# Attention weights times values as three passes of split operands, and negated scores whose minimum is taken, in a hybrid attention/GLA decoder trunk

## The chip, the cores and the metric

One core of one Trainium2 chip runs the whole program. The metric is the device time of one execution in microseconds (us), as the median over runs; smaller is better. Engine names are those of the profile: PE is the matrix engine, PEld its weight loads, DVE the vector engine, ACT the scalar engine, POOL and SP the other two.

## What is computed

Four residual layers over 1,040 tokens (16 learned meta tokens ahead of 1,024 real ones) of width 1,024 in float32: differential attention, squared-ReLU MLP, gated linear attention, MLP. The change touches the attention layer alone. Cut to that:

```python
def diff_attention(x, w_in, lam_params, subln_w, w_out, lambda_init):
    q, k, v = jnp.split(x @ w_in, [D_MODEL, 2 * D_MODEL], axis=-1)
    # 8 heads; q and k have two components of 64, v has 128 columns per head
    for s, e in bounds:          # 16 meta rows, then 8 blocks of 128 rows
        scores = jnp.einsum('bqhcd,bkhcd->bhcqk', qb, kb) * scale
        scores = jnp.where(dist >= 0.0, scores - slopes * dist, -jnp.inf)
        p = jax.nn.softmax(scores, axis=-1)
        attn = p[:, :, 0] - lam * p[:, :, 1]
        outs.append(jnp.einsum('bhqk,bkhe->bqhe', attn, vb))
    o = rmsnorm(o, subln_w) * (1.0 - lambda_init)
    return o.reshape(B, L, DA_HEADS * DA_V_DIM) @ w_out
```

## The kernel before, in words

The projections of a head (`att_project`, L385) are products in three passes of split operands: a float32 operand is kept as a rounded part in the type F32R and the F32R remainder, and `mm3` (L185) multiplies high by high, low by high and high by low, lines L190, L191 and L192, in chunks of 348, 346 and 346 columns. The scores of row block i (`Head.score`, i = 0 to 8) are two F32R passes per chunk, L421 and L422: K split into KH and KL, against Q with both halves of its split stacked in the 128 rows. A DVE custom instruction (L424) adds the distance table `nsd` and carries the running maximum; L428 negates the maximum; ACT takes the exponential with the sum beside it (L429); L433 to L435 combine the two components into `e`.

`Head.turn` then transposes `e` in blocks of 128 keys on PE (L453, four to a PSUM bank of the tag `tp`, which has two banks) and ACT copies each bank to a tile `pt` (L454). `Head.av` multiplies: for each key block one plain float32 product `pt` by `V` of 128x128 (L469), and one with the meta values `Vm` (L467), summed in the one bank of the tag `o`. Block i has i + 1 such products, so a head has 45 and the eight heads 360. DVE copies the result to `osb` (L473), ACT sums its squares (L474). After blocks 3 and 8, `norm` scales by the root mean square (L484), transposes back (L492) and spills a split copy to DRAM (`spill`, L393 to L396), to be read for the output projection.

The heads are pipelined. In the main loop each row block runs the steps "FSFSFAT": F is a third of a chunk of the next head's projection, S half of the scores, A the `av` of the block turned in the step before, T the next `turn`. The Tile framework then orders the instructions of every engine by itself, so rows of different lines interleave on PE. `turn` takes its `pt` tiles from the pool `tmp` of four buffers, which `norm` uses too.

The whole program is ordered in this way: attention until about 548 us of the span, the output projection, MLP (L1066, L898), GLA, MLP.

Of the kernel before, what the change touches and what calls it, by code (L numbers as in the profile page):

```python
# [8 lines left out]
F32 = mybir.dt.float32  # L9
# [7 lines left out]
P = 128  # L17
# [33 lines left out]
def tile_hybrid_trunk(ctx, tc, hT, win, lamp, wout, gwin, gwz, gwup, gwout, wup, wdn, wdl,  # L51
# [219 lines left out]
    def small_rs(ssq, add, cnt, lo, hi):  # L271
        w = mpool.tile([P, 16], F32, tag="nrm_w", name=nm("nw"))
        r = mpool.tile([P, 16], F32, tag="nrm_r", name=nm("nr"))
        t = mpool.tile([P, 16], F32, tag="nrm_t", name=nm("nt"))
# [12 lines left out]
        return r  # L287
# [79 lines left out]
        return KH, KL  # L367

    def turn_v(h, v):
        V = slot(16 + 8 * (h % 2) + 6, "V", F32, (P, 8, P))  # L370
        Vm = mpool.tile([P, P], F32, tag="vm", name=nm("vm"))
        nc.gpsimd.memset(Vm, 0.0)
        for g in range(2):
            tp = psum("tp")
            for j in range(4):
                kb = 4 * g + j
                nc.tensor.transpose(tp[:, j * P:(j + 1) * P], v[:, NMETA + kb * P:NMETA + (kb + 1) * P], ident)
            nc.scalar.copy(V[:, 4 * g:4 * g + 4, :].rearrange("p a b -> p (a b)"), tp)
        tp = psum("tp")
        nc.tensor.transpose(tp[:NMETA, :P], v[:, 0:NMETA], ident)  # L380
        nc.scalar.copy(Vm[:NMETA], tp[:NMETA, :P])
        return V, Vm

    def att_project(h, R):
        q = slot(32, "qst")  # L385
        yield from proj(xs, CH3, ev_scaled(q, 0.125), bank_pj, lambda: R.update(Q=split_q(h, q)), cuts=(3, 5))
# [11 lines left out]
    class Head:  # L398
        def __init__(self, h, R):
            self.h, self.R = h, R  # L400
            self.sums = mpool.tile([P, 2, 9], F32, tag="sums", name=nm("sums"))
            self.ssq = mpool.tile([P, 9], F32, tag="ssq", name=nm("ssq"))
            self.e, self.pt, self.osb = {}, {}, {}

        def score(self, i):
            if i == 0 and self.h > 0:
                nc.scalar.mul(nsd, nsd, 0.5)
            Q, (KH, KL), sums = self.R["Q"], self.R["K"], self.sums
            nk = NMETA + P * i
            off = 912 if i == 0 else 1024 - P * i  # L410
            q0 = 0 if i == 0 else NMETA + P * (i - 1)
            e = [slot(34 + 2 * (i % 3) + c, "e") for c in range(2)]
            st4 = mpool.tile([P, 16], F32, tag="mx", name=nm("mx"))
            mx = st4[:, 0:8].rearrange("p (c j) -> p c j", j=4)
            nmx, rho = st4[:, 8:10], st4[:, 10:12]
            chs = col_chunks(nk)
            for c in range(2):
                for j, (c0, n) in enumerate(chs):
                    ps = psum("s")
                    w = n  # L420
                    nc.tensor.matmul(ps[:, :w], Q[c][:, q0:q0 + P], KH[c][:, c0:c0 + w], start=True, stop=False)  # L421
                    nc.tensor.matmul(ps[:, :w], Q[c][:, q0:q0 + P], KL[c][:, c0:c0 + w], start=False, stop=True)  # L422
                    last = j == len(chs) - 1
                    nc.vector.tensor_tensor_reduce(  # L424
                        e[c][:, c0:c0 + n], ps[:, :n], nsd[:, off + c0:off + c0 + n], 1.0,
                        -3.0e38 if j == 0 else mx[:, c, j - 1:j], ALU.add, ALU.max,
                        mx[:, c, 3:4] if last else mx[:, c, j:j + 1])
                nc.vector.tensor_scalar(nmx[:, c:c + 1], mx[:, c, 3:4], -1.0, None, ALU.mult)  # L428
                nc.scalar.activation(e[c][:, :nk], e[c][:, :nk], AF.Exp, bias=nmx[:, c:c + 1],  # L429
                                     accum_out=sums[:, c, i:i + 1])  # L430
                if c == 0:
                    yield
            nc.vector.reciprocal(rho[:, 0:1], sums[:, 1, i:i + 1])  # L433
            nc.vector.scalar_tensor_tensor(rho[:, 1:2], sums[:, 0, i:i + 1], nlam, rho[:, 0:1], ALU.mult, ALU.mult)
            nc.vector.scalar_tensor_tensor(e[0][:, :nk], e[1][:, :nk], rho[:, 1:2], e[0][:, :nk],  # L435
                                           ALU.mult, ALU.add)
            self.e[i] = e[0]

        def turn(self, i):
            a = self.e.pop(i)  # L440
            blocks = [(NMETA + P * b, b) for b in range(i)] + [(0, -1)]
            res = []
            for g in range(0, len(blocks), 4):
                part = blocks[g:g + 4]
                tp = psum("tp")
                pt = tmp("pt")
                w = P * len(part)
                if i == 0:
                    nc.tensor.transpose(tp[:NMETA, :P], a[:, 0:NMETA], ident)
                    nc.scalar.copy(pt[:NMETA, :P], tp[:NMETA, :P])  # L450
# [4 lines left out]
                res += [(pt, j, b) for j, (_, b) in enumerate(part)]  # L455
            self.pt[i] = res

        def av(self, i):
# [1 line left out]
            res = self.pt.pop(i)  # L460
            o = psum("o")
            n = len(res)
            for d, (pt, j, b) in enumerate(res):
                s = slice(j * P, (j + 1) * P)
                if b < 0:
                    kr = NMETA if i == 0 else P
                    nc.tensor.matmul(o[:, :P], pt[:kr, s], Vm[:kr], start=d == 0, stop=d == n - 1)  # L467
                else:
                    nc.tensor.matmul(o[:, :P], pt[:, s], V[:, b, :], start=d == 0, stop=d == n - 1)  # L469
            g, lo = (0, 0) if i < 4 else (1, 4)  # L470
            if g not in self.osb:
                self.osb[g] = slot((23, 31)[g], "osb", F32, (P, 5, P))
# [6 lines left out]

        def norm(self, lo, hi):  # L480
            r = small_rs(self.ssq, self.sums[:, 0, :], P, lo, hi)
            ob = self.osb[lo // 4]
            for j in range(hi - lo):
                nc.vector.tensor_scalar(ob[:, j, :], ob[:, j, :], r[:, lo + j:lo + j + 1], None, ALU.mult)  # L484
            idx = list(range(lo, hi))
            while idx:
                part, idx = idx[:4], idx[4:]
# [1 line left out]
                w = 0  # L489
                for i in part:  # L490
                    m = NMETA if i == 0 else P
                    nc.tensor.transpose(tp[:, w:w + m], ob[:m, i - lo, :], ident[:m, :m])  # L492
                    w += m
                t0 = 0 if part[0] == 0 else NMETA + P * (part[0] - 1)
                ot = tmp("ot")
# [3 lines left out]
                        op0.new_o(7)  # L499
                    op0.put_o(7, ot, t0, w)  # L500
                else:
                    spill(osp[self.h], ot, ob.rearrange("p a b -> p (a b)")[:, :w] if lo == 0 or t0 == 400 else ob[:, 4, :], t0, w)

    q0t, k0t = slot(32, "qst"), slot(33, "kst")
    R0 = {}

# [11 lines left out]
    proj_k(lambda k: xs[k], CH3, [first_ev(ev_scaled(q0t, 0.125)), first_ev(ev_rs(k0t))], bank_any)  # L518
    for j, (ev, ps, c0, n) in enumerate(late):
        ev(ps, c0, n)  # L520
        if j == 2:
# [1026 lines left out]
def _layout(inputs):  # L1548
# [77 lines left out]
```

## Time and profile before

| what | value |
|---|---|
| median of 3 runs | 2405.39 us (2404.58 to 2406.35) |
| profiled execution, its own time | 2403.48 us |
| span of the profiled execution | 2401.6 us |
| PE busy | 2360.3 us, 98% of the span |
| PE weight loads busy | 2160.6 us, 90% |
| DVE busy | 1641.3 us, 68% |
| ACT busy | 1089.9 us, 45% |
| chain that ended last | PE 91%, DVE 5%, DMA 2%, ACT 1% |
| granted PE clock, mean | 0.997 |

The span is cut from the first to the last instruction; 1.9 us of the execution lie around it. A PE record's length runs from its start to its modelled end, and consecutive matmuls overlap in the array, so how fast PE works is read from start to start. A plain float32 product leaves two records of each kind (weight load, matmul), an F32R product and a transpose leave one. Busy time of a group is the union of its records.

### The profile page before, as it was taken

To read this page: it belongs to the slowest core of one execution; us is meant where nothing else is said; L and a number is where in the kernel's file an instruction comes from. 1 tells how busy PE (TensorE), PEld (TensorE's weight loads), DVE (VectorE), ACT (ScalarE), POOL (GpSimd) and SP (SyncE) were. 2 spreads that over 40 slices of the span, in tenths; PEclk is the share of its full clock that TensorE was granted. 3 is DMA by queue.
4 is the path that set the end of the run, shared out by engine and by line. 5 is a ranking of instruction groups with operands and counts; after the bars stand their busy time and mean duration, and the time that the engine had idled before them with its cause. 6 is when DMAs were issued, how large, how long until landed. Compare 5 with 4: busy or idle time off the path is not lost.

```text
span 2401.6 us, 38832 instructions
## 1 busy us (share of the span) xinstructions
PE 2360.3 (98%) x14862; PEld 2160.6 (90%) x14862; DVE 1641.3 (68%) x3552; ACT 1089.9 (45%) x2107; POOL 192.9 (8%) x146
## 2 busy tenths in 40 slices
PE   8999999999899999999999999999989999999998
PEld 8999999989899999999999898898868888888888
DVE  7777777767855656857656586685686666786765
ACT  5555555555534344544443334233544444454442
POOL 0000000000332220000000000000032222000000
PEclk9999999999999999999999999999999999999999
DMA  4122222334344447945552111123434444884553
GB/s 164 52 63 63 63 63 62 117 119 142 123 143 145 144 145 253 314 134 175 161 172 68 36 36 52 46 77 125 141 113 155 149 145 149 276 307 145 175 177 104
DMA packets 130826, 317.76 MB, mean 132 GB/s; under 512 B 14864, under 2 KB 22480, under 8 KB 130640
## 3 DMA queue, kind: packets, MB, share of 16 engines
q1 hardware_dynamic: 130640, 315.29, 39.9%
q8 instruction: 116, 1.90, 0.3%
q14 instruction: 70, 0.57, 0.1%
HBM read 219.04 MB, written 87.67 MB: 128 GB/s over the span
## 4 chain that ended last, share of the span: by engine, by line
PE 91%; DVE 5%; DMA 2%; ACT 1%; issue 1%; POOL 0%; SPq 0%; DVEq 0%; ACTq 0%; POOLq 0%
PE PS L898 26%; PE PS L1066 23%; PE PS L190 9%; PE PS L191 9%; PE PS L192 9%; PE PS L469 2%; PE PS L453 2%; PE PS L421 1%; PE PS L220 1%; PE PS L422 1%; PE PS L1378 1%; DVE KL L364 1%; DVE wop L230 1%; PE PS L467 1%; PE PS L1451 1%
## 5 line engine op out<-in xcount | busy, mean ns | idle before, releaser
L1066 PE MATMUL PS<-xop,wop 128*128 128x260 f32 (+1 forms) x4032 | 640.1, 321 | 13.8 <-ACT C L1128 4.4
L1066 PEld LDWEIGHTS PS<-xop,wop 128*128 128x128 f32 x4032 | 576.0, 188 | 77.6 <-ACT C L1128 5.7
L898 PE MATMUL PS<-xop,wop 128*128 128x260 f32 (+2 forms) x4224 | 637.8, 313 | 2.1 <-DVE C L1139 2.1
L898 PEld LDWEIGHTS PS<-xop,wop 128*128 128x128 f32 x4224 | 585.5, 189 | 53.7 <-DVE C L1139 2.3
L230 DVE TENSOR_TENSOR wop<-raw,wop 128x512 fp32r<-128x512 f32 x384 | 277.7, 727 | 214.8 <-ACT wop L229 213.9
L229 ACT CAST wop<-raw 128x512 fp32r<-128x512 f32 x384 | 235.1, 620 | 349.4 <-PE PS L898 103.8
L190 PE MATMUL PS<-xh,wh 128*128 128x346 f32 (+2 forms) x992 | 346.6, 350 | 0.0
L191 PE MATMUL PS<-xh,wl 128*128 128x346 f32 (+2 forms) x992 | 334.5, 337 | 0.3 <-DVE wl L171 0.3
L192 PE MATMUL PS<-xl,wh 128*128 128x346 f32 (+2 forms) x992 | 332.5, 335 | 0.0
L190 PEld LDWEIGHTS PS<-xh,wh 128*128 128x128 f32 x992 | 187.3, 189 | 7.9
L191 PEld LDWEIGHTS PS<-xh,wl 128*128 128x128 f32 x992 | 187.0, 189 | 8.1 <-DVE wl L171 0.6
L192 PEld LDWEIGHTS PS<-xl,wh 128*128 128x128 f32 x992 | 186.8, 188 | 7.3
L229 ACT CAST xop<-xr 128x520 fp32r<-128x520 f32 (+1 forms) x224 | 138.8, 621 | 77.9 <-DMA xr<-xd 60.0
L230 DVE TENSOR_TENSOR xop<-xr,xop 128x520 fp32r<-128x520 f32 (+1 forms) x224 | 153.3, 691 | 27.8 <-ACT xop L229 27.2
L429 ACT ACTIVATE e<-e,mx 128x16 f32<-128x16 f32 (+5 forms) x144 | 105.6, 735 | 82.9 <-DVE mx L428 82.9
L1101 ACT ACTIVATE C<-C 128x520 f32<-128x520 f32 (+1 forms) x128 | 81.2, 635 | 132.7 <-DVE C L1099 131.4
L170 ACT CAST wh<-raw 128x1024 fp32r<-128x1024 f32 (+2 forms) x64 | 65.3, 1021 | 156.2 <-PE PS L192 144.9
L424 DVE CUSTOM_DVE_ANT_0 e<-PS,nsd 128x16 f32<-128x16 f32 (+5 forms) x144 | 64.9, 459 | 76.2 <-PE PS L422 56.9
L191 PE MATMUL PS<-oh,wl 128*128 128x512 f32 (+2 forms) x320 | 113.1, 353 | 0.8 <-DVE wl L171 0.8
L192 PE MATMUL PS<-ol,wh 128*128 128x512 f32 (+2 forms) x320 | 112.7, 352 | 0.5 <-DMA ol<-osp 0.5
L190 PE MATMUL PS<-oh,wh 128*128 128x512 f32 (+2 forms) x320 | 112.4, 354 | 0.6 <-DMA oh<-osp 0.6
L1017 POOL TENSOR_TENSOR raw<-raw 128x512 f32<-128x512 f32 x32 | 48.1, 1504 | 525.2 <-ACT xop L229 414.7
(244 smaller groups left out, 3178.9 us busy)
## 6 DMA issues: line engine op xcount, KB each, us to landing
raw<-in_wdn_dram SPq DMA_DIRECT2D x104, 512.0 KB, 4.0
raw<-in_wup_dram SPq DMA_DIRECT2D x64, 512.0 KB, 4.1
xr<-xd SPq DMA_DIRECT2D x112, 260.0 KB, 3.6
xr<-xd SPq DMA_DIRECT2D x112, 256.0 KB, 3.7
xd<-T SPq DMA_DIRECT2D x64, 260.0 KB, 4.4
xd<-T SPq DMA_DIRECT2D x64, 256.0 KB, 4.1
xd<-C SPq DMA_DIRECT2D x48, 260.0 KB, 2.0
raw<-in_gwin_dram SPq DMA_DIRECT2D x24, 512.0 KB, 3.6
```

The costliest lines, as they stand in the source:

```text
L170: nc.scalar.copy(wh[:, :w], raw[:, :w])
L190: nc.tensor.matmul(ps[:, :n], wh[:, w0:w0 + P], xh[:, c0:c0 + n], start=j == 0, stop=False)
L191: nc.tensor.matmul(ps[:, :n], wl[:, w0:w0 + P], xh[:, c0:c0 + n], start=False, stop=False)
L192: nc.tensor.matmul(ps[:, :n], wh[:, w0:w0 + P], xl[:, c0:c0 + n], start=False, stop=j == len(xs) - 1)
L229: nc.scalar.copy(hi, src)
L230: nc.vector.tensor_sub(lo, src, hi.bitcast(F32))
L424: nc.vector.tensor_tensor_reduce(e[c][:, c0:c0 + n], ps[:, :n], nsd[:, off + c0:off + c0 + n], 1.0, -3.0e38 if j == 0 else mx[:, c, j - 1: ...
L429: nc.scalar.activation(e[c][:, :nk], e[c][:, :nk], AF.Exp, bias=nmx[:, c:c + 1], accum_out=sums[:, c, i:i + 1])
L898: nc.tensor.matmul(PS[:, b, :n], W[:, wo + wc:wo + wc + P], X[:, xo + c0:xo + c0 + n], start=kp == 0 and q == 0 and not more, stop=kp == N ...
L1017: nc.gpsimd.tensor_add(a21, a21, a22)
L1066: nc.tensor.matmul(ps[:, :n], o[:, wi + kp * P:wi + (kp + 1) * P], xi[:, c0:c0 + n], start=start and q == 0, stop=stop and q == 2, skip_gr ...
L1101: due.append((t + 1, lambda: nc.scalar.activation(h, h, AF.Square)))
```

## The change

The values are split into F32R halves `VH`, `VL` (and `Vm` into two), and the transposed weights into `hi`, `lo`: ACT writes the high part from PSUM, DVE subtracts it from the same PSUM bank. Each product becomes three F32R passes into the same bank. The copy of the result moves from DVE to ACT. Q and the distance table take the opposite sign, the running minimum replaces the maximum, and the exponential runs with scale -1, so that the negation goes. The second component of `e` has two buffers in place of three, which frees slot 39 for one result tile `OB` that all heads share; slots 23 and 31 hold the low halves of V. The third group of block 8 uses a tile `ptm` of its own.

```diff
 def turn_v(h, v):
-        V = slot(16 + 8 * (h % 2) + 6, "V", F32, (P, 8, P))
+        VH, VL = [slot(16 + 8 * (h % 2) + 6 + c, "V", F32R, (P, 8, P)) for c in range(2)]
+        Vm = mpool.tile([P, 2, P], F32R, tag="vm", name=nm("vm"))
+        def halves(hi, lo, ps):
+            nc.scalar.copy(hi, ps)
+            nc.vector.tensor_sub(lo, ps, hi.bitcast(F32))
...
 def score(self, i):
-            e = [slot(34 + 2 * (i % 3) + c, "e") for c in range(2)]
+            e = [slot(34 + i % 3, "e"), slot(37 + i % 2, "e")]
...
-                        -3.0e38 if j == 0 else mx[:, c, j - 1:j], ALU.add, ALU.max,
+                        3.0e38 if j == 0 else mx[:, c, j - 1:j], ALU.add, ALU.min,
...
-                nc.vector.tensor_scalar(nmx[:, c:c + 1], mx[:, c, 3:4], -1.0, None, ALU.mult)
-                nc.scalar.activation(e[c][:, :nk], e[c][:, :nk], AF.Exp, bias=nmx[:, c:c + 1],
+                nc.scalar.activation(e[c][:, :nk], e[c][:, :nk], AF.Exp, bias=mx[:, c, 3:4], scale=-1.0,
                                      accum_out=sums[:, c, i:i + 1])
...
 def turn(self, i):
-                pt = tmp("pt")
+                if g < 8:
+                    hi, lo = [tpool.tile([P, 520], F32R, tag="tmp", name=nm("pt")) for _ in range(2)]
+                else:
+                    hi, lo = [ptm[:, c, :] for c in range(2)]
...
-                    nc.scalar.copy(pt[:, :w], tp[:, :w])
+                nc.scalar.copy(hi[:m, :w], tp[:m, :w])
+                nc.vector.tensor_sub(lo[:m, :w], tp[:m, :w], hi[:m, :w].bitcast(F32))
...
 def av(self, i):
-                    nc.tensor.matmul(o[:, :P], pt[:, s], V[:, b, :], start=d == 0, stop=d == n - 1)
+                for q, (l, r) in enumerate(((hi, vh), (lo, vh), (hi, vl))):
+                    nc.tensor.matmul(o[:, :P], l[k, s], r, start=d == 0 and q == 0, stop=d == n - 1 and q == 2)
...
-            nc.vector.tensor_copy(self.osb[g][:, i - lo, :], o[:, :P])
+            nc.scalar.copy(o0 if i == 0 else OB[:, i - 1, :], o[:, :P])
             nc.scalar.activation(o[:, :P], o[:, :P], AF.Square, accum_out=self.ssq[:, i:i + 1])
...
+    OB = slot(39, "osb", F32, (P, 8, P))
+    ptm = mpool.tile([P, 2, P], F32R, tag="wg", name="ptm", bufs=1)
+    o0 = OB[:, 7, :]
...
-    dist = (-0.5 * np.where(dd >= 0, dd, 1e30)).astype(np.float32)
+    dist = (0.5 * np.where(dd >= 0, dd, 1e30)).astype(np.float32)
```

On PE, the end of a step and the turn of block 8 stood like this before: `av` of block 7 (L469 and L467, seven value blocks and the meta block), the nine transposes of block 8 (L453), and the projection that fills between them (L190 to L192).

```order
L469 MATMUL PS<-V_475,pt_1144 128x128 x4
L469 MATMUL PS<-V_475,pt_1150 128x128 x3
L467 MATMUL PS<-vm_476,pt_1150 128x128
L453 MATMUL PS<-ident,e_1006 128x128 x8
L190 MATMUL PS<-xh_117,wh_839 128x346
L191 MATMUL PS<-xh_117,wl_840 128x346
L192 MATMUL PS<-xl_118,wh_839 128x346
L453 MATMUL PS<-ident,e_1006 128x128
```

The same place now begins with 18 more rows like the first three (L477 is the product, L461 the transpose, `V_477` and `V_478` the two halves of V, `pt_1216` and `pt_1217` those of the weights):

```order
L477 MATMUL PS<-V_477,pt_1216 128x128
L477 MATMUL PS<-V_477,pt_1217 128x128
L477 MATMUL PS<-V_478,pt_1216 128x128
L477 MATMUL PS<-vm_479,pt_1216 128x128
L477 MATMUL PS<-vm_479,pt_1217 128x128
L477 MATMUL PS<-vm_479,pt_1216 128x128
L461 MATMUL PS<-ident,e_1040 128x128 x8
L190 MATMUL PS<-xh_117,wh_852 128x346
L191 MATMUL PS<-xh_117,wl_853 128x346
L192 MATMUL PS<-xl_118,wh_852 128x346
L190 MATMUL PS<-xh_123,wh_852 128x346
...
L461 MATMUL PS<-ident,e_1040 128x128
```

Eight float32 products became 24 F32R ones, every one with another stationary operand than its neighbour, and the ninth transpose moved from three projection rows behind the first eight to seven.

On DVE, around the scores of blocks 1 and 2 of the next head, the two score rows of a block now stand behind subtractions (L463) that did not exist before, and their negations are gone:

```order
L463 TENSOR_TENSOR pt_1209<-PS,pt_1208 128x512
L463 TENSOR_TENSOR pt_1217<-PS,pt_1216 128x512
L429 ISA e_1233,mx_1235<-PS,nsd 128x144
L429 ISA mx_1235 128x1
L429 ISA e_1234,mx_1235<-PS,nsd 128x144
...
L463 TENSOR_TENSOR pt_1290<-PS,pt_1289 128x512
L463 TENSOR_TENSOR pt_1298<-PS,pt_1297 128x512
L463 TENSOR_TENSOR ptm<-PS,ptm 128x128
L429 ISA e_1317,mx_1319<-PS,nsd 128x272
```

The subtraction reads the `tp` bank after ACT's copy of it, so a bank is now released by DVE instead of by ACT, and a score reduction queued behind it waits for that copy too.

## Rows read from the trace of the kernel before

**Rows 1.** The page, busy time, share of the span and instructions of each engine.

```profile
PE 2360.3 (98%) x14862; PEld 2160.6 (90%) x14862; DVE 1641.3 (68%) x3552; ACT 1089.9 (45%) x2107; POOL 192.9 (8%) x146
```

**Rows 2.** Busy time by stretch: one middle head, and most of the last head.

```profile
core 0: us, PE busy (x) PEld busy (x) DVE busy (x) ACT busy (x) POOL busy (x), PEclk, DMA share, GB/s
...
308.00:371.00 63.00, 62.74 (x432) 60.27 (x431) 44.69 (x154) 35.56 (x91) 0.20 (x1) 1.00 0.21 60
...
496.00:540.00 44.00, 42.30 (x292) 38.86 (x291) 30.29 (x116) 24.78 (x69) 0.00 (x0) 1.00 0.16 53
```

**Rows 3.** Who PE waited for between 57 and 548 us: total, times, longest.

```profile
PE PS L421 <- DVE mx L424: 2.2, 8, 0.6
PE PS L190 <- DMA oh<-osp: 0.6, 1, 0.6
PE PS L192 <- DMA ol<-osp: 0.5, 1, 0.5
PE PS L469 <- ACT PS L474: 0.4, 1, 0.4
```

**Rows 4.** Groups by line and shape on PE, 0 to 1200 us: the value products.

```profile
L469 PE MATMUL PS<-V,pt 128*128 128x128 f32 x576 | 78.6, 277 | 0.4 <-ACT PS L474 0.4
...
L467 PE MATMUL PS<-vm,pt 128*128 128x128 f32 x128 | 24.8, 275 | 0.0
...
L467 PE MATMUL PS<-vm,pt 16*128 16x128 f32 x16 | 3.9, 321 | 0.0
```

**Rows 5.** The chain that ended last, one `av` of block 7: start, length, what.

```profile
302.55 1.56 PE PS L469 x14
304.11 0.22 PE PS L467 x2
```

**Rows 6.** Timeline, two F32R passes of 16 columns between wide ones: start, length.

```profile
104.02 0.19 PEld L421 LDWEIGHTS PS<-KH,Q 128*128 128x128 f32 x1
...
104.18 0.17 PE L421 MATMUL PS<-KH,Q 128*128 128x16 f32 x1
104.18 0.19 PEld L422 LDWEIGHTS PS<-KL,Q 128*128 128x128 f32 x1
104.20 0.26 PE L422 MATMUL PS<-KL,Q 128*128 128x16 f32 x1
...
104.29 0.19 PEld L190 LDWEIGHTS PS<-xh,wh 128*128 128x128 f32 x1
104.31 0.41 PE L190 MATMUL PS<-xh,wh 128*128 128x348 f32 x1
104.40 0.19 PEld L191 LDWEIGHTS PS<-xh,wl 128*128 128x128 f32 x1
104.56 0.33 PE L191 MATMUL PS<-xh,wl 128*128 128x348 f32 x1
104.56 0.19 PEld L192 LDWEIGHTS PS<-xl,wh 128*128 128x128 f32 x1
104.72 0.32 PE L192 MATMUL PS<-xl,wh 128*128 128x348 f32 x1
```

**Rows 7.** Timeline, two F32R passes of 144 columns.

```profile
110.89 0.23 PE L421 MATMUL PS<-KH,Q 128*128 128x144 f32 x1
...
110.96 0.28 PE L422 MATMUL PS<-KL,Q 128*128 128x144 f32 x1
```

**Rows 8.** Groups on DVE, 57 to 548 us.

```profile
L428 DVE TENSOR_SCALAR mx<-mx 128x1 f32<-128x1 f32 x140 | 20.7, 149 | 1.6
L473 DVE COPY osb<-PS 128x128 f32<-128x128 f32 x72 | 20.5, 285 | 20.8 <-PE PS L467 19.3 <-PE PS L421 0.9
...
L230 DVE TENSOR_TENSOR ot<-ot,osb 128x512 fp32r<-128x512 f32 x7 | 4.8, 687 | 0.0
```

**Rows 9.** Groups on ACT, 57 to 496 us.

```profile
L454 ACT COPY pt<-PS 128x512 f32<-128x512 f32 x56 | 31.1, 581 | 13.1 <-PE PS L453 13.0
```

**Rows 10.** DMA issues of the spill: KB each, median us from issue to landing.

```profile
osp<-osb SPq DMA_DIRECT2D x7, 200.0 KB, 1.9
```

More of the change, by code (lines that the diff above doesn't have):

```diff
@@ L273, in small_rs @@
         r = mpool.tile([P, 16], F32, tag="nrm_r", name=nm("nr"))
-        t = mpool.tile([P, 16], F32, tag="nrm_t", name=nm("nt"))
+        t = mpool.tile([P, 16], F32, tag="nrm_t", name=nm("nt"), bufs=1)
         sl = slice(lo, hi)
@@ L377, in turn_v @@
                 nc.tensor.transpose(tp[:, j * P:(j + 1) * P], v[:, NMETA + kb * P:NMETA + (kb + 1) * P], ident)
-            nc.scalar.copy(V[:, 4 * g:4 * g + 4, :].rearrange("p a b -> p (a b)"), tp)
+            halves(*[V[:, 4 * g:4 * g + 4, :].rearrange("p a b -> p (a b)") for V in (VH, VL)], tp)
         tp = psum("tp")
         nc.tensor.transpose(tp[:NMETA, :P], v[:, 0:NMETA], ident)
-        nc.scalar.copy(Vm[:NMETA], tp[:NMETA, :P])
-        return V, Vm
+        halves(Vm[:NMETA, 0, :], Vm[:NMETA, 1, :], tp[:NMETA, :P])
+        return (VH, VL), Vm
     def att_project(h, R):
         q = slot(32, "qst")
-        yield from proj(xs, CH3, ev_scaled(q, 0.125), bank_pj, lambda: R.update(Q=split_q(h, q)), cuts=(3, 5))
+        yield from proj(xs, CH3, ev_scaled(q, -0.125), bank_pj, lambda: R.update(Q=split_q(h, q)), cuts=(3, 5))
         k = slot(33, "kst")
@@ L402, in __init__ @@
             self.ssq = mpool.tile([P, 9], F32, tag="ssq", name=nm("ssq"))
-            self.e, self.pt, self.osb = {}, {}, {}
+            self.e, self.pt = {}, {}
         def score(self, i):
@@ L445, in turn @@
                 tp = psum("tp")
-                pt = tmp("pt")
                 w = P * len(part)
+                if g < 8:
+                    hi, lo = [tpool.tile([P, 520], F32R, tag="tmp", name=nm("pt")) for _ in range(2)]
+                else:
+                    hi, lo = [ptm[:, c, :] for c in range(2)]
+                m = P
                 if i == 0:
+                    m = NMETA
                     nc.tensor.transpose(tp[:NMETA, :P], a[:, 0:NMETA], ident)
-                    nc.scalar.copy(pt[:NMETA, :P], tp[:NMETA, :P])
                 else:
@@ L462, in av @@
             n = len(res)
-            for d, (pt, j, b) in enumerate(res):
+            for d, (hi, lo, j, b) in enumerate(res):
                 s = slice(j * P, (j + 1) * P)
[L465 to L468, printed above, removed]
-                    nc.tensor.matmul(o[:, :P], pt[:, s], V[:, b, :], start=d == 0, stop=d == n - 1)
-            g, lo = (0, 0) if i < 4 else (1, 4)
-            if g not in self.osb:
-                self.osb[g] = slot((23, 31)[g], "osb", F32, (P, 5, P))
-            nc.vector.tensor_copy(self.osb[g][:, i - lo, :], o[:, :P])
+                k = slice(0, NMETA if i == 0 else P)
+                vh, vl = (Vm[k, 0, :], Vm[k, 1, :]) if b < 0 else (V[0][:, b, :], V[1][:, b, :])
+                for q, (l, r) in enumerate(((hi, vh), (lo, vh), (hi, vl))):
+                    nc.tensor.matmul(o[:, :P], l[k, s], r, start=d == 0 and q == 0, stop=d == n - 1 and q == 2)
+            nc.scalar.copy(o0 if i == 0 else OB[:, i - 1, :], o[:, :P])
             nc.scalar.activation(o[:, :P], o[:, :P], AF.Square, accum_out=self.ssq[:, i:i + 1])
@@ L481, in norm @@
             r = small_rs(self.ssq, self.sums[:, 0, :], P, lo, hi)
-            ob = self.osb[lo // 4]
-            for j in range(hi - lo):
-                nc.vector.tensor_scalar(ob[:, j, :], ob[:, j, :], r[:, lo + j:lo + j + 1], None, ALU.mult)
+            ob = {i: o0 if i == 0 else OB[:, i - 1, :] for i in range(lo, hi)}
+            flat = OB.rearrange("p a b -> p (a b)")
+            for i, t in ob.items():
+                nc.vector.tensor_scalar(t, t, r[:, i:i + 1], None, ALU.mult)
             idx = list(range(lo, hi))
@@ L501, in norm @@
                 else:
-                    spill(osp[self.h], ot, ob.rearrange("p a b -> p (a b)")[:, :w] if lo == 0 or t0 == 400 else ob[:, 4, :], t0, w)
+                    c0 = 3 * P if part[0] == 4 else 0
+                    spill(osp[self.h], ot, flat[:, c0:c0 + w], t0, w)
+    OB = slot(39, "osb", F32, (P, 8, P))
+    ptm = mpool.tile([P, 2, P], F32R, tag="wg", name="ptm", bufs=1)
+    o0 = OB[:, 7, :]
     q0t, k0t = slot(32, "qst"), slot(33, "kst")
```

11 lines of the change are left out of this document (5 added, 6 removed).

## The prediction

> **What bounds the kernel now.** I read the page first: PE is busy 98% of the span, the next engine 68% [rows 1]. A share over the whole span says little of one stage, so I next took the busy times by stretch. One head of the attention lasts 63 us; in a middle one PE is busy 62.74 us, DVE 44.69 and ACT 35.56, at a granted clock of 1.00 [rows 2], which is the 2.4 GHz level. The list of PE's waits confirms it: between 57 and 548 us PE waited 2.2 + 0.6 + 0.5 + 0.4 = 3.7 us in all [rows 3]. So through the whole attention PE is the bound. What shortens another engine can give back at most these 3.7 us, and whatever is added to PE is added to the end. The question is what PE pays for the value products, before and after.
>
> **Before.** A product leaves two matmul records; 576 + 128 + 16 = 720 records are 360 products [rows 4], 45 a head. The means there (277 ns) are no price, since records overlap. The chain of waits gives it from start to start: 14 records of L469 take 1.56 us and two of L467 0.22 [rows 5], so 1.78 / 16 = 0.111 us a record, 0.223 us a product, 80 us in all.
>
> **After.** 1,080 F32R passes, one record each, with 128 columns and a stationary operand that changes at every pass. The trace has no F32R pass of 128 columns, so I bound it by the nearest ones.
>
> - The low end is streaming alone: of two 144-column passes the second starts 0.07 us after the first [rows 7]; at 128 columns that is 0.07 x 128 / 144 = 0.062 us.
> - The high end is a weight load for each. With only 16 columns to stream, weight loads start at 104.18, 104.29 and 104.40, 0.11 us apart [rows 6]. The second 16-column matmul does start 0.02 us behind the first, because its weights had been loaded under the wide pass ahead; but the debt is paid at once. From the first narrow matmul (104.18) to L191 (104.56) two narrow and one wide pass take 0.38 us; a wide one alone takes 0.16 (104.56 to 104.72). The two narrow ones cost 0.22 together, 0.11 each, although they stream almost nothing.
>
> In an `av` of up to 27 passes in a row no wide matmul covers the loads, so I take 0.11 us a pass. A split product then costs 0.33 us where the float32 one cost 0.223: the two records of the float32 product already ran at the pace of two weight loads, and the change makes it three. That is one more load for each of 360 products: **360 x 0.11 = +39.6 us**, 5.0 us a head, all of it on PE.
>
> The Trainium skill, page "TensorE: Matmul & The Clock Gate", section "Back-to-back issue gap", gives about 81 ns a matmul for a sustained stream of load and matmul pairs at 128 columns. By it the sum would be, as an estimate, 360 x (3 x 0.081 - 0.223) = +7 us. The trace does not agree for this type: 0.11 us between loads even at 16 columns [rows 6].
>
> **What lies beside PE.** DVE gains, per head, 15 subtractions in `turn` over 45 blocks of 128 columns and three for V. I price them by the 512-wide subtraction, 0.687 us, and the 128-wide copy, 0.285 us [rows 8]: (0.687 - 0.285) / 384 = 1.05 ns a column and 0.15 us each; 5,760 columns in 15 instructions give 8.3 us, V gives 1.7. It loses 18 negations of 0.149 and nine copies of 0.285, 5.3 us [rows 8]. Net +4.7 us: 44.7 becomes 49.4 us, of a head that PE stretches to 68. That costs nothing as long as PE is the bound; the share of DVE rises from 71% to 73%. ACT takes over nine copies of about 0.27 us (as the DVE copy), 2.4 us, and has room (35.6 of 63). POOL clears a `Vm` twice as wide, once a head, and is idle otherwise. The shorter chain from score to exponential takes 0.15 us off a path that PE does not wait on; against it the second pass of `av` needs the subtraction, which is ready a step (63 / 9 = 7 us) earlier. Both at nothing; were DVE late, PE would stand at L477 in `av` or at L426 for a bank of scores.
>
> The shared `OB` puts a wait on ACT's queue: the spill of blocks 0 to 3 reads 400 columns, the last 16 of which are the first of block 4's place, so the copy of block 4 waits for that transfer, 1.9 us from issue to landing [rows 10]. That copy comes a step of 7 us after block 3's; the exponentials queued behind it have room. The same holds for the four `tmp` buffers: the second low half of block 4 takes the buffer of `norm`'s spilled tile, and on DVE some nine instructions stand between. I take nothing for either.
>
> A `tp` bank is now released by copy and subtraction, 0.581 + 0.687 = 1.27 us [rows 8, 9], where the copy's 0.58 did. Block 8 needs a third bank while there are two. The order puts seven projection passes of 0.16 us (1.1 us) and four transposes of 0.11 (0.4 us) between, 1.5 us, so it is about covered; uncovered, with DVE busy on something else, up to 1.5 us in each of eight heads, 12 us. I take nothing in the middle heads. The last head has no projection of a next one to fill with: PE stood idle there for 44 - 42.3 = 1.7 us [rows 2], and I let that double: +1.7.
>
> **The sum.** 39.6 + 1.7 = 41.3 us on the profiled execution: 2403.5 + 41.3 = 2444.8. That execution was 1.9 us below the median of the runs shown, so the forecast on the median is **2447 us**, 1.7% slower. Low end: all 3.7 us of waits go, and the first pass of each of 72 `av` finds its weights loaded, 72 x 0.05 = 3.6 us less, and no idle time is added: 2405.4 + 39.6 - 7.3 = 2438. High end: the 12 us at the banks come on top: 2459.
>
> **Rivals.**
>
> 1. *Faster: the weight load does not set the pace of a row of F32R passes.* If it streams at 0.062 us, three passes cost 0.186 us against 0.223: 360 x -0.037 = -13 us, 2392. It decides at 0.223 / 3 = 0.074 us a pass. For it: 0.07 us between two passes [rows 7]. Against it: that pair had its load paid by the neighbours, and [rows 6] show the bill. The Trainium skill, same page, section "Weight-path perf modes", says that a fast weight load is on for 128 weights of any type but FP32; it would make this rival true if F32R counted as another type, and the 0.11 us between loads [rows 6] speak against it. Chance 0.04.
> 2. *Much slower: the split starves PE.* The subtraction sits in DVE's queue ahead of the score reductions, ACT's copy ahead of it; if PE then waits 0.7 us (the subtraction) at each of the 64 turns of blocks 1 to 8, 45 us come on top, half of it 22: 2461 to 2492. For it: DVE at 73%, banks that are held twice as long. Against it: PE waited for DVE for 2.2 us in 491 us [rows 3] with nearly the same load. Chance 0.09.
> 3. *Nothing: the passes fall into idle time of PE.* Against it: 0.26 us of idle time in a head of 63 [rows 2], where 5 us are wanted. Time 2405. Chance 0.02.
> 4. *A little slower*, a pass between the two bounds, 0.08 us: 360 x (0.24 - 0.223) = +6 us, 2412. Chance 0.02.
>
> **How the numbers follow.** The forecast has 0.83. The range takes its two ends and a little for the median's own scatter: 2437 to 2460; outside lie the rivals with 0.17 together. A measurement of this kernel tells about 0.2% (5 us) from no change. Faster by more: 0.04. Within: 0.02. Slower by more: 0.83 + 0.09 + 0.02 = 0.94.
>
> **What would show it.** In the new profile a row of L477 passes should start every 0.11 us, 24 of them about 2.7 us in the chain of waits; the stretch of a middle head should grow from 63 to 68 us with PE still at 99% and DVE near 49 us; PE's waits on DVE and ACT before 590 us should stay under 15 us. Passes 0.08 us apart or less make the forecast wrong downwards; a PE that waits at L461, L477 or L426 for more than 15 us, upwards. The time after the attention should not change.

## The result, and the profile after

| | before | the change |
|---|---|---|
| median | 2405.87 us (2404.58 to 2407.81, 4 runs) | 2502.65 us (2496.52 to 2506.34, 4 runs) |
| ratio | | 1.0399, 95% interval 1.0377 to 1.0421 |
| profiled execution, own time | 2403.48 us | 2503.35 us |
| mean granted PE clock | 0.997 | 0.990 |

The change is slower by 97 us, where 41 were forecast, and the time lies far above the range. The page of the change, with the lines that answer to [rows 1]:

```profile
span 2501.6 us, 39574 instructions
...
PE 2424.4 (97%) x15222; PEld 2214.6 (89%) x15222; DVE 1688.0 (67%) x3480; ACT 1111.1 (44%) x2179; POOL 196.0 (8%) x146
...
PE 83%; DVE 10%; ACT 3%; issue 2%; DMA 1%; POOL 0%; SPq 0%; DVEq 0%; ACTq 0%
```

PE's busy time grew by 64 us and the span by 100: a third of the loss is time in which PE does nothing. On the chain that ended last PE holds 83% where it held 91, and DVE 10% where it held 5. Busy time by stretch, of a head as long as it is now, answers to [rows 2] and has its columns:

```profile
184.00:258.00 74.00, 68.58 (x474) 64.75 (x473) 50.58 (x145) 37.37 (x100) 0.31 (x1) 1.00 0.17 51
```

A head repeats every 74 to 75 us now, every 63 before, so some 12 us more for each of eight heads: this is nearly the whole loss. PE is busy 68.6 us of it, 5.8 more than before, close to the 5.0 us that the third weight load was to cost. But it stands idle for 5.4 us, where it stood for 0.26. DVE is busy for 50.6 of 74 us, 68%, a smaller share than before. It isn't full; it is late. PE's waits, as [rows 3] showed them:

```profile
PE PS L498 <- DVE osb L490: 17.2, 14, 1.5
PE PS L426 <- DVE mx L429: 10.9, 10, 1.5
PE PS L385 <- DVE V L376: 8.5, 7, 1.2
...
PE PS L461 <- DVE vm L376: 1.7, 3, 0.6
...
PE PS L477 <- DVE pt L463: 0.8, 3, 0.4
PE PS L477 <- ACT pt L462: 0.7, 1, 0.7
```

39.8 us in place of 3.7, at the same places in head after head: twice before the transposes of the scaled result (L498, after blocks 3 and 8), once before a score bank (L426), once before the bank for the transposed meta values (L385).

The price of a pass is on the timeline, at block 8 of a head, and behind it the first of these waits:

```profile
206.32 2.51 PE L477 MATMUL PS<-V,pt 128*128 128x128 f32 x21
...
207.33 1.22 DVE L171 TENSOR_TENSOR wl<-raw,wh 128x1024 fp32r<-128x1024 f32 x1
...
208.58 1.24 DVE L354 TENSOR_TENSOR Q<-qst,Q 64x1040 fp32r<-64x1040 f32 x1
208.67 0.50 PE L477 MATMUL PS<-vm,ptm 128*128 128x128 f32 x3
209.00 0.37 PE L190 MATMUL PS<-xh,wh 128*128 128x348 f32 x1
...
209.85 1.24 DVE L355 TENSOR_TENSOR Q<-qst,Q 64x1040 fp32r<-64x1040 f32 x1
...
211.12 0.17 DVE L280 TENSOR_SCALAR nw<-ssq 128x5 f32<-128x5 f32 x1
...
212.60 1.07 DVE L490 TENSOR_SCALAR osb<-osb,nr 128x128 f32<-128x128 f32 x5
212.94 0.52 PE L498 MATMUL PS<-ident,osb 128*128 128x128 f32 x2 [1.45 <-DVE osb L490]
```

24 passes start in 209.00 - 206.32 = 2.68 us, 0.112 each: the forecast price. The wait is another matter. The product ends at 209.0, its result is scaled from 212.6 on, because L171, L354 and L355 stand ahead on DVE and the small steps of the norm (from L280 on) come behind them. DVE was not quicker before. The same place in the kernel before, with its last product, the scaling and the first transpose:

```profile
185.58 0.39 PE L467 MATMUL PS<-vm,pt 128*128 128x128 f32 x2
...
191.61 1.07 DVE L484 TENSOR_SCALAR osb<-osb,nr 128x128 f32<-128x128 f32 x5
...
191.96 0.33 PE L492 MATMUL PS<-ident,osb 128*128 128x128 f32 x1
```

From the last product to the scaling it was 191.61 - 185.58 = 6.03 us there and is 212.60 - 208.67 = 3.93 us now, and yet PE did not wait: 37 projection and score matmuls stood on PE between the product and the transposes of the result. Now it is 14, and PE is through with them 1.45 us too early. In PE's order:

```
L477 MATMUL PS<-vm_479,ptm 128x128 x3
L190 MATMUL PS<-xh_117,wh_1139 128x348
...
L192 MATMUL PS<-xl_136,wh_1139 128x348
L498 MATMUL PS<-ident,osb_166 128x128 x2
```

The second kind of wait, for a score bank, on the same view 25 us later:

```profile
231.33 2.50 DVE L364 TENSOR_TENSOR KL<-kst,KH 64x1040 fp32r<-64x1040 f32 x2
...
233.86 0.69 DVE L463 TENSOR_TENSOR pt<-PS,pt 128x512 fp32r<-128x512 f32 x1
234.46 0.56 DVE L429 CUSTOM_DVE_ANT_0 e<-PS,nsd 128x392 f32<-128x392 f32 x1
...
235.08 0.45 PE L426 MATMUL PS<-KH,Q 128*128 128x392 f32 x1 [1.23 <-DVE mx L429]
```

The new subtraction (L463) and the K subtractions stand ahead of the score reduction that would free the bank.

The idle stretches have a follower: the granted clock. Busy time by stretch around one of them:

```profile
100.00:108.80 8.80, 7.43 (x51) 6.60 (x49) 7.42 (x22) 5.21 (x8) 0.00 (x0) 0.99 0.01 2
108.80:112.40 3.60, 3.60 (x19) 3.60 (x18) 2.42 (x5) 2.04 (x7) 0.00 (x0) 0.55 0.28 97
112.40:120.00 7.60, 7.60 (x60) 7.60 (x59) 2.29 (x10) 2.34 (x9) 0.00 (x0) 1.00 0.06 23
```

After 1.4 us of idle time in 8.8 the next 3.6 us have a granted clock of 0.55, so PE runs for most of them at the lower level, 1.2 GHz, and is back after that. The granted clock in the stretches from 57 to 720 us is 0.97 to 0.99 in several and 0.91 from 533 to 590 us; shortfall times length comes to about 14 us there. Before, no stretch of the attention was under 1.00.

So of 97 us, 40 are the third load, 36 are waits (39.8 - 3.7), up to 14 the clock; some 7 have no name. The experiments ask what makes the waits.

### The profile page after: what moved, and what is told of

It reads as the page before. It is cut to its first block, busy times and chain, and to the rows that moved or that the text cites. A ratio compares the mean times of both kernels' runs of the same rounds, so it can differ in the third digit from the quotient of the medians.

```text
span 2501.6 us, 39574 instructions
## 1 busy us (share of the span) xinstructions
PE 2424.4 (97%) x15222; PEld 2214.6 (89%) x15222; DVE 1688.0 (67%) x3480; ACT 1111.1 (44%) x2179; POOL 196.0 (8%) x146
## 4 chain that ended last, share of the span: by engine, by line
PE 83%; DVE 10%; ACT 3%; issue 2%; DMA 1%; POOL 0%; SPq 0%; DVEq 0%; ACTq 0%
PE PS L1076 24%; PE PS L908 24%; PE PS L190 8%; PE PS L191 8%; PE PS L192 8%; PE PS L477 3%; DVE e L429 2%; PE PS L461 2%; PE PS L220 1%; PE PS L1388 1%; ACT e L433 1%; PE PS L427 1%; PE PS L426 1%; DVE wl L171 1%; DVE wop L230 1%
## 5 line engine op out<-in xcount | busy, mean ns | idle before, releaser
L190 PE MATMUL PS<-xh,wh 128*128 128x346 f32 (+2 forms) x992 | 347.7, 351 | 0.0
L192 PE MATMUL PS<-xl,wh 128*128 128x346 f32 (+2 forms) x992 | 331.5, 334 | 0.0
L190 PEld LDWEIGHTS PS<-xh,wh 128*128 128x128 f32 x992 | 188.2, 190 | 8.2
L192 PEld LDWEIGHTS PS<-xl,wh 128*128 128x128 f32 x992 | 187.0, 189 | 7.3
L477 PE MATMUL PS<-V,pt 128*128 128x128 f32 x864 | 112.9, 278 | 1.1 <-ACT pt L462 0.7
L192 PE MATMUL PS<-ol,wh 128*128 128x512 f32 (+2 forms) x320 | 113.0, 353 | 0.0
L190 PE MATMUL PS<-oh,wh 128*128 128x512 f32 (+2 forms) x320 | 112.4, 354 | 0.0
L477 PEld LDWEIGHTS PS<-V,pt 128*128 128x128 f32 x864 | 109.9, 197 | 2.7 <-ACT pt L462 1.6
```

Source lines behind the costliest of these rows:

```text
L190: nc.tensor.matmul(ps[:, :n], wh[:, w0:w0 + P], xh[:, c0:c0 + n], start=j == 0, stop=False)
L192: nc.tensor.matmul(ps[:, :n], wh[:, w0:w0 + P], xl[:, c0:c0 + n], start=False, stop=j == len(xs) - 1)
L477: nc.tensor.matmul(o[:, :P], l[k, s], r, start=d == 0 and q == 0, stop=d == n - 1 and q == 2)
```

## The experiments

Two theories for them. The **order theory**: the framework lays the instructions of each engine down in another order once the product is made of narrow F32R passes, and in this order PE reaches its consumers before DVE has served them. The **work theory**: the subtractions and the PSUM banks held by them make DVE late.

**One part alone: everything but the product.** Opposite sign, minimum, `OB`, two buffers for the second component and the copy on ACT stay; the product is a plain one again.

```diff
-                nc.vector.tensor_sub(lo[:m, :w], tp[:m, :w], hi[:m, :w].bitcast(F32))
...
-                for q, (l, r) in enumerate(((hi, vh), (lo, vh), (hi, vl))):
-                    nc.tensor.matmul(o[:, :P], l[k, s], r, start=d == 0 and q == 0, stop=d == n - 1 and q == 2)
+                nc.tensor.matmul(o[:, :P], hi[k, s], Vm[k] if b < 0 else V[:, b, :], start=d == 0, stop=d == n - 1)
```

> The change without its product: plain float32 value products on unsplit weights and values, all the rest kept (opposite sign and minimum, two buffers for the second score component, one shared result tile, result copied by ACT). Two theories for the 97 us: 40 us are the third weight load of 360 products; of the other 57 us the order theory says that they come from the order in which the instructions were laid down (the transposes of the result stand 14 rows behind the product instead of 36, so PE reaches them before they are ready), the work theory that they come from the added subtractions on DVE and the PSUM banks that these hold. Here both expect the time of before, 2400 to 2411 us. If the shared result tile or the moved copy is what stalls, it shows here: over 2425 us.

2404.63 us beside 2405.49, ratio 0.9992 (0.9983 to 1.0001). The negation that went, the shared result tile and the moved copy cost nothing and bring nothing that can be measured, as forecast.

**Three passes, no subtraction.**

```diff
-                nc.vector.tensor_sub(lo[:m, :w], tp[:m, :w], hi[:m, :w].bitcast(F32))
...
-                for q, (l, r) in enumerate(((hi, vh), (lo, vh), (hi, vl))):
+                for q, (l, r) in enumerate(((hi, vh), (hi, vh), (hi, vh))):
```

> Three passes per product as in the change, but no subtraction: the low halves of the weights and of the values are neither made nor used, all three passes multiply the high halves (this leaves the low halves out of the computation). PE's work is that of the change, DVE's is less than before. The work theory expects before + 40 = 2441 to 2452 us and PE's waits in the attention under 10 us. The order theory, whose transposes still stand 14 to 16 rows behind the product here, expects the two waits of about 1.4 us a head to stay: 2463 to 2485 us.

2474.82 us, ratio 1.0288 (1.0271 to 1.0306), inside what the order theory expected. PE's waits:

```profile
PE PS L496 <- DVE osb L488: 13.8, 14, 1.4
PE PS L425 <- DVE mx L428: 10.5, 10, 1.3
PE PS L475 <- ACT pt L461: 2.0, 3, 0.9
PE PS L384 <- ACT V L375: 1.5, 7, 0.2
```

Two of the three kinds stay with DVE relieved of all new work; the one for the transpose bank goes from 8.5 to 1.5 us. 40 us of passes and 28 of waits, less the 3.7 of before, make 64 of the 69 measured. The subtractions are worth 28 us in this order.

**All subtractions, plain product.**

```diff
-                for q, (l, r) in enumerate(((hi, vh), (lo, vh), (hi, vl))):
-                    nc.tensor.matmul(o[:, :P], l[k, s], r, start=d == 0 and q == 0, stop=d == n - 1 and q == 2)
+                nc.tensor.matmul(o[:, :P], hi.bitcast(F32)[k, s], vh.bitcast(F32), start=d == 0, stop=d == n - 1)
```

> All halves are made as in the change, with all subtractions, but the product is one plain float32 product of the high halves (the low halves are left out of the product). DVE's and ACT's work and the buffers are those of the change, PE's that of before; the transposes of the result stand 29 to 34 rows behind the product. The work theory expects 2440 to 2465 us; the order theory 2400 to 2415 us; the third weight load is absent for both.

2406.77 us, ratio 1.0009 (1.0000 to 1.0019). The whole of DVE's and ACT's new work hides under a PE that has only its old work, in an order near the old one (transposes 29 to 37 rows behind the product); the score bank, for one, costs next to nothing:

```profile
PE PS L476 <- ACT PS L478: 2.2, 2, 1.6
...
PE PS L426 <- DVE mx L429: 1.1, 6, 0.3
```

The work theory by itself falls here.

**Two passes.**

```diff
-                for q, (l, r) in enumerate(((hi, vh), (lo, vh), (hi, vl))):
+                for q, (l, r) in enumerate(((hi, vh), (lo, vh))):
```

> The change with its third pass left out (high weights by low values), so two F32R passes a product, 720 weight loads as before. If a pass costs a weight load, this takes 40 us off the change: 2460 to 2466 us with all stalls unchanged. The order theory expects more off, since half of the transposes now stand 23 rows behind instead of 15: 2430 to 2455 us. If passes were cheap after all and the stalls everything, it stays above 2480 us.

2457.10 us, ratio 1.0218 (1.0203 to 1.0233). The third pass was worth 45 us. What remains is the telling number: two narrow passes are PE's old work to a per cent (two loads at 0.112 us), and still the kernel is 51 us slower than before. Its waits:

```profile
PE PS L498 <- DVE osb L490: 21.5, 14, 2.5
PE PS L385 <- DVE V L376: 7.5, 7, 1.2
PE PS L426 <- DVE mx L429: 7.1, 10, 0.9
```

The time is 2 us above what the order theory expected, and that theory in its simple form (count the matmuls at this one place) missed. The transposes after block 3 stand 23 matmuls behind the product here instead of 15 and wait 0.94 us where they waited 1.21; those after block 8 stand 14 behind as in the change, and wait 2.45 us where they waited 1.45. The order has to be taken as a whole, with what stands ahead of the result on DVE.

**Only the order of the transposes.** `norm` is cut in two, and its second half (transposes, copy, spill) is called one step later in the program, before the next `av`.

```diff
+            late_norm.append(lambda: self.norm_b(lo, hi, ob))
+
+        def norm_b(self, lo, hi, ob):
...
                 elif step == "A" and turned:
+                    run_late()
                     o, j = turned.pop(0)
```

> The change, with the transposes of the normed result and what follows them written one step later in the program, so that they stand 29 to 37 rows behind the product as before the change. Order theory: the waits of PE for the scaled result (17 to 22 us) go, and some half-clock stretches with them: 2470 to 2486 us. If the order of these transposes does not matter, 2496 to 2506 us.

2487.21 us, ratio 1.0338 (1.0322 to 1.0353): 15 us off the change with the same instructions, a microsecond short of the expectation. The wait at the transposes is gone (0.7 us), but others have grown into its place:

```profile
PE PS L432 <- DVE mx L435: 13.8, 16, 1.2
PE PS L385 <- DVE V L376: 12.5, 7, 1.8
PE PS L467 <- ACT ot L511: 6.1, 6, 1.0
...
PE PS L507 <- DVE osb L495: 0.7, 1, 0.7
```

**Three repairs at once.**

```diff
-            nc.vector.tensor_sub(KL[c][a], k[a], KH[c][a].bitcast(F32))
+            nc.gpsimd.tensor_sub(KL[c][a], k[a], KH[c][a].bitcast(F32))
...
+        tp = psum("tp")
+        nc.tensor.transpose(tp[:NMETA, :P], v[:, 0:NMETA], ident)
+        halves(Vm[:NMETA, 0, :], Vm[:NMETA, 1, :], tp[:NMETA, :P])
         for g in range(2):
```

> As the run with the later transposes, and in addition the meta values are transposed ahead of the two groups of V and the low half of K is subtracted on POOL instead of DVE. If the rest of the stalls are the other two waits of each head (for a score bank behind the K subtraction, for a transpose bank behind the V subtraction, together about 20 us), 2447 to 2468 us, the bare price of the third weight load being 2445. If they only move elsewhere, 2468 to 2490 us.

2480.17 us, ratio 1.0308 (1.0291 to 1.0324). The second expectation held: the waits mostly moved, from 40 us to about 28. Repairing single places does not cure the lateness.

**One wide pass, one narrow.** High weights meet high and low values side by side, 256 columns behind one load.

```diff
+                vv = Vm[k] if b < 0 else V[b // 4][:, b % 4]
+                nc.tensor.matmul(o[:, :2 * P], hi[k, s], vv.rearrange("p a b -> p (a b)"), start=d == 0, stop=d == n - 1,
+                                 skip_group_check=True)
+                nc.tensor.matmul(o[:, :P], lo[k, s], vv[:, 0, :], start=False, stop=d == n - 1,
+                                 skip_group_check=True)
...
+            nc.scalar.copy(dst, o[:, P:2 * P])
+            nc.vector.tensor_add(dst, o[:, :P], dst)
```

> The change with the first and the third pass made one: high weights by high and low values side by side, 256 columns behind one weight load, then low weights by high values; the two halves are added on DVE when the result is copied. Weight loads per product: two, as before. If the load sets a pass's pace, a product costs 0.12 + 0.11 = 0.23 us (260 columns take 0.12), and the order laid down for it has the transposes 27 to 36 rows behind: 2405 to 2416 us. If streaming sets it, three times 128 columns cost what they did and the time stays over 2440 us.

2430.84 us, ratio 1.0108 (1.0091 to 1.0125). The same arithmetic as the change, 72 us faster, and still 25 above before; I had expected at most 11. Streaming does not set a pass's pace: the columns are the same 384, and of the 72 us only 24 are waits. Those are down, but the ones at the result's transposes are still there:

```profile
PE PS L502 <- DVE osb L494: 10.6, 13, 1.4
```

**Two wide passes.**

```diff
-                nc.tensor.matmul(o[:, :P], lo[k, s], vv[:, 0, :], start=False, stop=d == n - 1,
+                nc.tensor.matmul(o[:, :2 * P], lo[k, s], vv.rearrange("p a b -> p (a b)"), start=False, stop=d == n - 1,
```

> The run with one wide and one narrow pass, its narrow pass (low weights by high values, 128 columns) made 256 columns wide too, so that it also adds low by low: two weight loads a product, more columns, all subtractions kept. Its laid-down order has the transposes 33 to 40 rows behind the product throughout, that of the narrower kernel 27 to 36. Order theory: passes 360 x (2 x 0.12 - 0.223) = +6 us and hardly a stall: 2409 to 2419 us, faster than the 2431 us of the kernel that streams less. If order is not what matters: 2432 to 2440 us.

2419.15 us, ratio 1.0057 (1.0040 to 1.0074), at the upper edge of the order theory's number. More columns to stream, and 12 us faster:

```profile
PE PS L502 <- DVE osb L494: 3.5, 8, 1.5
```

Beside the run with two narrow passes the loads are equal, the columns double, the DVE work is one addition larger per block, and the time is 38 us shorter.

**Three wide passes.**

```diff
+                w2 = vv.rearrange("p a b -> p (a b)")
+                nc.tensor.matmul(o[:, :2 * P], lo[k, s], w2, start=False, stop=d == n - 1, skip_group_check=True)
+                nc.tensor.matmul(o[:, 2 * P:], hi[k, s], w2, start=d == 0, stop=d == n - 1, skip_group_check=True)
```

> Three passes a product, each with 256 columns (high and low values side by side), the third into columns that nobody reads: more work for PE than in the change, three loads and twice the columns, all subtractions kept, and one addition more on DVE. The order that is laid down has the transposes 27 to 37 rows behind the product. Order theory: no stalls beyond the passes, 3 x 0.12 - 0.223 = 0.137 us for 360 products, 49 us: 2450 to 2462 us, faster than the change although it does more. Work theory: at least as slow as the change, 2505 to 2520 us.

2460.82 us, ratio 1.0230 (1.0215 to 1.0246). Twice the columns of the change and an addition on top, and 42 us faster. Its third pass opens a sum of its own in the bank of the first two, and its result is not that of the layer; why was not looked into. A run further down has three wide passes with the change's own result and takes 52 us more than before where this one takes 55. All of PE's waits from 57 to 660 us come to 6.1 us; the largest:

```profile
PE PS L503 <- DVE osb L495: 3.7, 7, 1.0
```

Passes of 49 us and 2 us more of waits than before make 51 of the 55 measured: with three loads and without the narrow passes the forecast's kind of sum closes to 4 us.

**One narrow pass.**

```diff
+                nc.tensor.matmul(o[:, :P], hi[k, s], vv[:, 0, :], start=d == 0, stop=d == n - 1,
+                                 skip_group_check=True)
```

> One F32R pass of 128 columns a product, high by high (the low halves of weights and of the sum are left out; the copied result is added to itself so that DVE keeps that addition). One weight load where the kernel before has two, and an order with the transposes 34 to 40 rows behind the product. If a load is the price of a narrow pass, 360 x (0.11 - 0.223) = -40 us: 2363 to 2374 us. If a pass streams at 0.062 us, 2405 - 58 = 2345 to 2352 us. If narrow passes bring stalls by themselves, whatever the order, 2380 to 2400 us.

2383.15 us, ratio 0.9907 (0.9892 to 0.9922), 23 us under before, in the range of "narrow passes bring stalls by themselves". By the price of a load, one less takes 40 us off PE; the waits are 14 us where 3.7 were, although the transposes stand 34 to 40 matmuls behind the product:

```profile
PE PS L499 <- DVE osb L491: 6.1, 7, 1.0
PE PS L426 <- DVE mx L429: 4.3, 8, 0.6
```

Up to here waits come with narrow passes. Whether the chip stalls on narrow passes, or on the order that the framework lays down for them, is still open. The last three runs separate the two.

**Three wide passes with the change's own result.** The partner of the next run: every pass 256 columns wide, all three into the same columns, no addition.

```diff
+                vl = vv[:, 1:2, :].broadcast_to([vv.shape[0], 2, P]) if WIDE[0] else vv[:, 1, :]
+                vh = vv if WIDE[0] else vv[:, 0, :]
...
+                for q, (l, r) in enumerate(((hi, vh), (lo, vh), (hi, vl))):
```

> Three passes of 256 columns per product with the change's result in the first 128 columns: high x [VH|VL], low x [VH|VL], high x [VL|VL], all into the same columns; the copy on ACT is the change's, no addition. The framework lays the order down as it does for wide passes. Both theories: the passes cost 49 us over before (0.12 us each) and the waits are those of the other run with three wide passes, about 6, so 2455 to 2465 us. This kernel is the partner of the next one.

2457.71 us beside 2406.05, ratio 1.0213 (1.0198 to 1.0228). Waits 5.6 us. The price of a wide pass stands in its chain of waits, 2.48 / 21 = 0.118 us:

```profile
318.75 2.48 PE PS L481 x21
```

**Narrow passes in the wide order.** The program lays the wide kernel down first, reads its order, and states it for the narrow one, each instruction behind the one before it on its engine.

```diff
+    order = [number[i.name] for f in n0.m.functions for b in f.blocks for i in b.instructions if i.name in number]
+    WIDE[0] = False
...
+            if i.engine in last:
+                tc.add_manual_dep(i, last[i.engine].name, _mybir.DependencyInfo(
+                    _mybir.DependencyClass.NoSync, _mybir.DependencyReason.DATA), reason="order of the wide passes")
+            last[i.engine] = i
```

> The change's arithmetic, three passes of 128 columns, in the order of its partner with three wide passes: the partner is laid down first, and its order on TensorE, VectorE and ScalarE is then stated instruction by instruction, without semaphores of its own. Order theory: the waits of the change (40 us) fall to some 6 to 12, and the time is before + 40 for the third load + these = 2450 to 2462 us, at or under the partner. If narrow passes stall the chip by themselves, whatever the order: waits near 40 and 2485 us or more.

2454.49 us, ratio 1.0203 (1.0187 to 1.0218): the change's arithmetic with its 3 narrow passes, 48 us faster than the change. In the traces its rows follow the partner's one for one, 15,222 on PE, and so on DVE, ACT and POOL. All of PE's waits from 57 to 660 us come to 9.3 us, the largest:

```profile
PE PS L503 <- DVE osb L495: 4.9, 7, 0.8
PE PS L426 <- DVE mx L429: 1.5, 8, 0.3
PE PS L481 <- DVE pt L463: 1.4, 1, 1.4
```

At the product of block 8 shown above, the timeline of this kernel reads:

```profile
197.42 0.50 PE L481 MATMUL PS<-vm,ptm 128*128 128x128 f32 x3
...
201.35 1.07 DVE L495 TENSOR_SCALAR osb<-osb,nr 128x128 f32<-128x128 f32 x5
...
201.69 0.33 PE L503 MATMUL PS<-ident,osb 128*128 128x128 f32 x1 [0.79 <-DVE osb L495]
```

From the last three passes to the scaling it is 201.35 - 197.42 = 3.93 us, in the change 212.60 - 208.67 = 3.93 us: DVE needs exactly as long. But PE has 18 matmuls to do in the meantime and not 14, and waits 0.79 us, not 1.45.

**Wide passes in the narrow order.** The reverse, with the same few lines.

> The reverse: three passes of 256 columns in the order that the framework lays down for three narrow ones, stated instruction by instruction. Order theory: waits of 30 to 40 us come with the order, on top of passes worth 49 us, and the granted clock may fall as it did in the change: 2485 to 2515 us. If the order does not matter: like the partner with wide passes in their own order, 2455 to 2465 us.

2499.30 us, ratio 1.0389 (1.0372 to 1.0407), 42 us slower than the same wide passes in their own order. In the traces its rows follow those of the change one for one, and the change's waits are back at the change's places, 38.4 us in all:

```profile
PE PS L503 <- DVE osb L495: 15.5, 14, 1.3
PE PS L426 <- DVE mx L429: 9.8, 11, 1.3
PE PS L385 <- DVE V L376: 7.7, 7, 1.1
```

Together, against the kernel before of the same chip (passes by 0.112 us narrow, 0.12 wide; waits from PE's list in the attention, 3.7 of them in the kernel before; the 0.8 us for `wl` in the output projection is not counted):

| product | time to before, us | passes | waits |
|---|---|---|---|
| plain, subtractions kept | +1 | 0 | 6 |
| one narrow | -23 | -40 | 14 |
| two narrow | +51 | 0 | 41 |
| two wide | +13 | +6 | 7 |
| one wide, one narrow | +25 | +3 | 16 |
| three narrow (the change) | +97 | +40 | 40 |
| three narrow, no subtraction | +69 | +40 | 28 |
| three narrow, order of three wide | +48 | +40 | 9 |
| three wide, a sum more | +55 | +49 | 5 |
| three wide, same sum | +52 | +49 | 5 |
| three wide, order of three narrow | +93 | +49 | 38 |

For three passes this settles it: the waits come with the laid-down order, whatever the width of the passes, and the framework lays down the one order for 128 columns and the other for 256. The order is worth 48 us with narrow passes and 42 with wide ones, the width 3 us in either order. For one and two narrow passes the order was not exchanged; one narrow pass has waits of 14 us with its transposes as far behind as before, and whether those come from its order or from a PE with less to do is open. What passes and waits (less the 3.7 of before) leave over is 93 - 49 - 35 = 9 us in the last row, 21 in the change's row, up to 14 of them the clock, 14 for two narrow passes, 10 for one wide and one narrow, 7 for one narrow and 5 or less in the others; no row names it. Why the framework orders narrow passes so was not tried. None of these kernels beats the kernel before with the whole computation; the change without its product equals it.

## Why the prediction was wrong, by its steps

- *What bounds the kernel, and the price of the product*: right. A pass takes 0.112 us (0.11 forecast), 40 us in all; the run without the third pass is 45 us faster, in an order without the waits the change stands at +48, of which 40 are the load and 5 are what waits remain above before.
- *Both at nothing* (DVE's subtractions, ACT's copy): right for the work as such, which hides in the run with the plain product (+1 us).
- *"I take nothing in the middle heads"*: this step failed. I took PE's 3.7 us of waits [rows 3] as a property of the load on DVE, which hardly changes, and carried it over. It was a property of the order, which work stands how far ahead of its consumer: the same three passes in another order wait 9 us and not 40, and take 48 us less. The order of the change was there to be read, and I compared it at two places, the third bank of block 8 and the subtractions ahead of the scores; the transposes of the result, 36 or 37 matmuls behind the product before and 14 or 15 after, I did not compare. They are the largest wait, 17.2 us.
- *The banks*: named rightly, mis-sized. At the high end I gave 12 us to the third bank of block 8, which does not appear among the waits; the bank of the meta values (L385, 8.5 us) and the score bank (L426, 10.9) do. Of the signs, the limit of 15 us on all waits was broken (39.8), but the lines that I named for a miss upwards, L461, L477 and L426, hold only 14.1 of them; the largest, L498, was not on the list.
- *The lower clock* was in no term: up to 14 us, an estimate, that follow the idle stretches.
- *Rival 2* was the right sign and, at its upper price of 45 us, nearly the right size (36 of waits), though the time lies above its range too, and its lower end is off: half of 45 us on top of 2447 is 2469, not 2461. Its place was wrong, a short wait at each of 64 turns where the trace has long ones at four places a head. Its reason, a starved DVE queue, was half right: without the subtractions 28 of the 40 us of waits remain. It got a chance of 0.09 on the strength of the waits before, the same mistake.
- *Rival 1* falls: a wide pass costs no more load than a narrow one, and the narrow one isn't cheaper than 0.11. The Trainium skill's rule on fast weight loads ("TensorE: Matmul & The Clock Gate", "Weight-path perf modes") does not show for this type: 24 passes in 2.68 us.

## What to carry to other kernels

Where a stationary operand changes at every matmul, count weight loads, not columns: an F32R pass of 128 columns costs the 0.11 us of its load, one of 256 costs 0.12, so a split operand is cheaper with its halves side by side behind one load (72 us here, part of it waits; it did not beat the plain float32 product). A PE that never waits is a fact of the laid-down order as much as of the loads: when a change replaces PE instructions by others, compare for every consumer on PE how many instructions now stand between it and its producer, and what stands ahead of that producer on its own engine, before carrying the old waits over; an order that was lost can be stated as dependencies without semaphores, here worth 48 us. And when many small waits in a PE-bound stage appear, look whether the granted clock fell behind them.

## What was not expected of the hardware

Doubling the columns of every pass made the kernel faster twice (2457 to 2419 us, 2503 to 2461). Stretches with 1.4 us of idle time in 8.8 were followed by 3.6 us at a granted clock of 0.55, once in two heads, although PE was busy for most of the time before; the kernel before shows none in its attention. Idle time alone does not decide it: the wide passes in the narrow order wait nearly as long (38 us), and their granted clock from 57 to 627 us is 1.00, where the change's is 0.98. The wide passes first, then the change:

```profile
57.00:627.00 570.00, 531.12 (x3596) 496.78 (x3596) 390.91 (x1120) 289.68 (x765) 1.87 (x6) 1.00 0.20 63
57.00:627.00 570.00, 528.60 (x3570) 498.02 (x3569) 389.49 (x1119) 290.51 (x764) 1.87 (x6) 0.98 0.20 63
```

The change's row leaves 21 us over and that of the wide passes in its order 9; the 12 between them fit the 14 read from the stretches, but what the lower clock cost the change stays an estimate.
